# Later lists, the last two chunks sum by sum, and the entrance of Mamba-2 in the kernel of the 304 token columns

## The chip, the cores and the metric

The kernel is one launch on one core of a Trainium2 chip. The metric is device time in microseconds (us), the median of the runs shown. The engines are named as the profile names them: PE (the matrix engine; PEld is its weight load), DVE (vector), ACT (activations and casts), POOL (GpSimd) and SP (which issues DMAs).

## The reference

One inference step of a two-layer trunk: RWKV-7, then PEER, then Mamba-2, then PEER, each added to the residual h. A prompt of 256 tokens with 16 meta tokens ahead and 8 samples of 4 tokens share the weights, so 304 columns go through. All is float32; D is 1024. The parts that the change touches: per token and head, PEER takes 16 of 128 keys in two halves (`P_TOPK`), then 16 of their sums, each one of 16384 experts; in Mamba-2 (`ssd`), `Lmat` is what the kernel calls the score tiles E:

```python
def peer_ffn(xn, w_q, sub_keys, u_tab, v_tab):
    ...
    q = (xt @ w_q).reshape(T, P_HEADS, 2, P_QDIM // 2)
    s = jnp.einsum('thzd,zhkd->thzk', q, sub_keys).astype(F32)
    sv, si = lax.top_k(s, P_TOPK)     
    cand = sv[:, :, 0, :, None] + sv[:, :, 1, None, :]
    ...
    top_s, pos = lax.top_k(cand.reshape(T, P_HEADS, P_TOPK * P_TOPK), P_TOPK)
    eidx = jnp.take_along_axis(cand_idx.reshape(T, P_HEADS, P_TOPK * P_TOPK), pos, axis=-1)
    gate = jax.nn.softmax(top_s, axis=-1).astype(xn.dtype)
    ...
        u = u_tab[i_blk]
        v = v_tab[i_blk]
        act = jax.nn.gelu(jnp.einsum('td,ted->te', x_blk, u), approximate=False)
        return jnp.einsum('te,ted->td', g_blk * act, v)

def ssd(x, dt, A, Bm, Cm, h0, lead_pad, chunk):
    ...
    adt = jnp.moveaxis(dt * A, 2, -1)
    Lmat = jnp.exp(segsum(adt))
    cb = jnp.einsum('bclgn,bcsgn->bcgls', Cm, Bm)
    y_diag = jnp.einsum('bcgls,bcgrls,bcsgrp->bclgrp', cb, Lmat, xdt)
    decay_st = jnp.exp(a_cs[..., -1:] - a_cs)
    ...
```

## The kernel before

**Layout.** The residual is h[128, 8, 304]: 8 blocks of 128 features, 304 token columns. `trunk` runs rwkv, peer of layer 0, mamba and peer of layer 1 one after the other. The two peer phases are recorded in a block that the scheduler orders by a simulated timeline, and Mamba-2's instructions can also be emitted in another order than written; what is passed to `keep_in_program_order` stays in the order of the code with its like.

**Products.** Every float32 product is split in a high part (cast) and a remainder. `load_w` (L293) fetches 128x1024 weights into `wraw` (3 buffers); `split` (L276) has ACT cast them to `whi` (L279), and the remainder `wlo` is taken by POOL (L284) for the first `leng` of 8 blocks and by DVE (L286) for the rest; `whi` and `wlo` have two buffers each. `mm3` (L301) issues 16 products, whi by the high and the low part of x in turn (L305, L306), and then 8 of wlo by the high part (L308), all into one sum. In the rows, `psc` is the sum of a u product, `xh` and `xl` the two parts of x.

**PEER.** All 16384 experts are computed for the 256 prompt tokens, in 128 u products of 256 columns (`s_chunk`, L1075), each with a Gelu on ACT. Beside the first 56 of them (B0) runs the selection `topk` on DVE, one step after each u product and two after every other: token group 0 (samples and meta), then 1 and 2 (128 prompt tokens each). Its rows bear the name G, since its scratch lies in that tensor: MAX8 at L993, the elementwise steps at L1007 to L1009, the sums at L1016 and L1017. The three last steps of a group are held in `late` and issued after the u product that a table names:

```python
        AFTER = ((14, 16, 55), (29, 31, 39), (46, 46, 52))
        for b in range(B0):
            s_chunk(b, G[:, b], leng=LP if b < LB else None, tag="so"[b % 2])
            next(tk, None)
            ...
                    if b == AFTER[ti][i]:
                        late[ti][i]()
```

These are `exps` (ACT, L1019), `gates` (DVE, L1022 to L1024), and for the prompt groups `finish`: three transposes `ptk` on PE (L1029) and a copy to the list `sel` on ACT; for group 0 it is `indices`, which writes the lists out by DMA. All 56 u products take the whole remainder on POOL (LP = 8).

**One-hots.** Then, for four tokens at a time, `onehots` (L1104) makes `oa` (on ACT, POOL or DVE by a pattern of letters) and `ob` (DVE, L1109) from `sel`, three buffers deep, so three groups can be made ahead; PE multiplies them (`pwt`, L1135) into the gates by expert, and DVE and ACT multiply G by these (L1136, L1137). Ten more u products are threaded through.

**v.** 128 chunks follow (L1248). Each has 12 products of 512 columns (L1288) into four sums `acc0` to `acc3`: sum i is token half i // 2 and feature half i % 2. Within a chunk come whi by gh (the high part of G) for the four sums, whi by glo, and wlo by gh; in chunk 127 the twelve are sorted by sum. At the end of layer 0 each sum is copied (ACT for even i, DVE for odd i), transposed on PE (`pot`, L1314) and added to h on DVE; in layer 1 the sums are normed and written out.

**Mamba-2.** `mamba` (L1321) fetches three blocks of the input weights (40, 32, 36). `pre` (L1351) splits two of them ahead with `load_w`, whose remainders go to POOL as a whole (LE = 8). `prenorm` (L333) makes xh and xl from h before the norm's factor is known (xl on DVE, L339), and then calls `rmsnorm` (squares on ACT and DVE, L319; the factor `rr`, L329), in whose middle block 40 is multiplied. `decays` makes from it the running sums of log decays (a chain on DVE), `ec` (L1472), whose product is `pcd`, and the 24 score tiles (L1482 to L1495): `rh` on POOL (L1489), two products `pe` on PE (L1492, and L1493 with the mask `mk`) and Exp on ACT (L1494). The projections and convolutions (`xc`, with Silu on ACT) run between them. `mk` is cast on DVE in two pieces: the identity at L1340 and the two masks at L1418.

Of the kernel before, what the change touches and what calls it, by code (L numbers as in the profile page):

```python
# [23 lines left out]
F32 = mybir.dt.float32  # L24
F32R = mybir.dt.float32r
# [12 lines left out]
KB = 8  # L38
# [28 lines left out]
def chain(*gens):  # L67
    for g in gens:
        yield from g
# [157 lines left out]
class K:  # L227
# [102 lines left out]
        for k in range(KB) if out is not None else ():  # L330
            nc.vector.scalar_tensor_tensor(out[:, k], h[:, k], self.vec(g, k), ri, op0=ALU.mult, op1=ALU.mult)

    def prenorm(self, out, h, g, xh, xl, sq, rr, tag, mid):  # L333

        nc = self.nc
        for k in range(KB):
            x = nc.scalar.activation(xh[:, k], h[:, k], AF.Copy, scale=self.vec(g, k))
            self.tc.keep_in_program_order(x)
            nc.vector.scalar_tensor_tensor(xl[:, k], h[:, k], self.vec(g, k), xh[:, k].bitcast(F32), op0=ALU.mult, op1=ALU.subtract)  # L339
        self.rmsnorm(out, h, g, sq, None, tag, rr, mid)  # L340
        return rr[1]

# [508 lines left out]
    def peer(self, l, ng):  # L851

        nc, tc, a, C, V = self.nc, self.tc, self.a, self.C, self.nc.vector
# [67 lines left out]
        for ti, slot in ((1, B0 + 8), (2, B0 + 16), (0, B0)):  # L921
            c0, c1 = TS[ti]
            n = c1 - c0
# [132 lines left out]
        def gather_u(gs):  # L1056

            for g in gs:


                xr = hs[:, 512 + 1024 * (g % 2):1536 + 1024 * (g % 2)]
                nc.sync.dma_start(xr, xd[16 * g:16 * g + 16, None, :].to_broadcast([16, 8, D]))
                yield
                for m in range(16):
                    rows = gview(slot(), (128, D))
                    nc.gpsimd.indirect_dma_start(out=rows, out_offset=None, in_=a[f"un{l}"],  # L1066
                                                 in_offset=bass.IndirectOffsetOnAxis(ap=gi[:, 0, g, m:m + 1], axis=0))
                    late_u.append((rows, xr, g, m))
                    if len(late_u) > LG:
                        dot(*late_u.pop(0))  # L1070
                    yield
            for x in late_u:
                dot(*x)
# [13 lines left out]

        tk = chain(topk(0), topk(1), topk(2))

        AFTER = ((14, 16, 55), (29, 31, 39), (46, 46, 52))  # L1090
        for b in range(B0):
            s_chunk(b, G[:, b], leng=LP if b < LB else None, tag="so"[b % 2])
            next(tk, None)
# [142 lines left out]
        def slot():  # L1236
# [5 lines left out]
            used[r] = now[1]  # L1242
            return 4 * r

        ggen = chain(gather_u(range(ng)), gather())
        nleft = 128 - B0 - NF
        done = 0
        for b in range(128):  # L1248
# [32 lines left out]

            vhf, vlf = (w.rearrange("p k d -> p (k d)") for w in (vh, vl))
            todo = [(i, g, w) for g, w in ((gh, vhf), (gl, vhf), (gh, vlf)) for i in range(4)]
            if b == 127:
                todo.sort(key=lambda x: x[0])
            for i, g, w in todo:
                t0, d0 = i // 2 * 128, i % 2 * 512
                mm(acc[i], lhsT=g[:, t0:t0 + 128], rhs=w[:, d0:d0 + 512], start=b == 0 and g is gh and w is vhf,  # L1288
# [14 lines left out]
        for i, pt in enumerate(self.gpt):  # L1303
            hk = self.h[:, 4 * i:4 * i + 4, 0:16 * ng].rearrange("p k (g t) -> p k g t", t=16)
            V.tensor_add(hk, hk, pt.rearrange("p k (g t) -> p k g t", t=32)[:, :, 0:ng, 0:16])
        for i in range(4):
            ot = gview(100 + 2 * i, (128, 512))
            if i % 2:
                V.tensor_copy(ot, acc[i])
            else:  # L1310
                nc.scalar.copy(ot, acc[i])
            pt = self.bank([128, 4, 128], "pot", "s")
            for j in range(4):
                mm(pt[:, j], lhsT=ot[:, j * 128:(j + 1) * 128], rhs=C["eye"], is_transpose=True, start=True, stop=True)  # L1314
            t0 = 48 + i // 2 * 128
            hk = self.h[:, i % 2 * 4:i % 2 * 4 + 4, t0:t0 + 128]
            V.tensor_add(hk, hk, pt)
# [3 lines left out]
    def mamba(self):  # L1321
# [15 lines left out]
        tok = pp.tile([128, 3, 128], F32, name="tok")  # L1337
        cdb = pp.tile([128, 10, 32], F32, name="cdb")
        mk = pp.tile([128, 3, 128], BF, name="mk")
        V.tensor_copy(mk[:, 2], C["eye"])  # L1340
        self.psum(i=2, G=2, f=2, t=2)
        ep = st.enter_context(tc.tile_pool(name="ep", bufs=4, reuse_waits="tile"))

# [4 lines left out]
        LE = 8  # L1348
        NU = 4
        done = [0]  # L1350
        pre = {b: self.load_w(a["win"][b], leng=LE, raw=raws[b]) for b in (40, 32)}  # L1351
        xn = ep.tile([128, KB, T], F32, name="xn", tag="E")
        rr = ep.tile([128, 2, T], F32, name="rr", tag="E")

        def proj(blk):

            if done[0] and blk == 40:
                return first.pop()
            w = pre.pop(blk) if blk in pre else self.load_w(a["win"][blk], leng=LE if done[0] < LM else None,
                                                                    raw=raws.get(blk))  # L1360
            c0 = M0 if blk < 16 else 0
            p = self.bank([128, T - c0], "pi", "i" if done[0] % NU < 2 or done[0] >= NU else "f")
            if done[0] == NU:
                with tc.high_priority(offset=200):
                    for k in range(KB):
                        self.split(xh[:, k], xl[:, k], xn[:, k])
            done[0] += 1
            self.mm3(p, w, (xh[:, :, c0:], xl[:, :, c0:]))
            return p

        first = []
        ri = self.prenorm(xn, self.h, "nm1", xh, xl, ep.tile([128, KB, T], F32, name="sq", tag="E"), (rr[:, 0], rr[:, 1]), "t",
                          lambda: first.append(proj(40)))
        gp = st.enter_context(tc.tile_pool(name="mg", bufs=2, reuse_waits="tile"))

        def conv(blk):
# [32 lines left out]
        def decays(dp):  # L1409
# [6 lines left out]
            x = t384("x"); xs = t384("xs")[:, 0:T]  # L1416
            V.tensor_mul(xs, p, ri)
            tc.keep_in_program_order(V.tensor_copy(mk[:, 0:2], nm))  # L1418
            p = xs
            for dst, src in ((x[:, 0:96].rearrange("p (c t) -> p c t", t=32), p[:, None, 16:48].to_broadcast([128, 3, 32])),  # L1420
                             (x[:, 96:128], p[:, 0:32]), (x[:, 128:384], p[:, 48:T])):
# [298 lines left out]
```

## Time and profile before

| | |
|---|---|
| median of 3 runs | 2630.28 us (2629.93 to 2636.83) |
| profiled execution | 2634.19 us, span 2632.3 us |
| granted TensorE clock, mean | 0.974 |
| busy PE | 2477.9 us (94%) |
| busy PEld | 2137.4 us (81%) |
| busy DVE | 1898.8 us (72%) |
| busy ACT | 1253.6 us (48%) |
| busy POOL | 1008.2 us (38%) |
| DMA | 460.34 MB, 175 GB/s over the span |

A share is busy time by the span, an average over stages with different limits. Rows of the trace give the start in us from the span's beginning, the duration, engine, line, operation, output <- inputs (buffer numbers left out), sizes, and how many alike follow each other (x8; the duration is then the sum); in brackets stands how long the engine had waited just before, and for which instruction. Rows of the waits give the total in us, how many and the longest.

### The profile page before, as it was taken

What the parts mean: (1) busy time and instruction counts of PE and PEld (TensorE: products, weight loads), DVE (VectorE), ACT (ScalarE), POOL (GpSimd) and SP (SyncE); (2) the same over time, 40 slices, a digit from 0 to 9 for tenths busy, and PEclk for the clock granted to TensorE, in tenths of its full rate; (3) what the DMA queues carried; (4) which work ended last, traced back from release to release, by engine and by line L of the source; (5) the groups of instructions that cost most, each with busy time, mean ns of one, the idle gap of its engine ahead of it and who ended that gap; (6) DMA issues with size and microseconds to landing.
All of it is one profiled execution on the core that took longest, in us unless ns stands there. A gap on an engine that the chain in (4) does not pass through costs nothing. (4 is left out here: it accounts for less than half of the span.)

```text
span 2632.3 us, 47459 instructions
## 1 busy us (share of the span) xinstructions
PE 2477.9 (94%) x18281; PEld 2137.4 (81%) x18281; DVE 1898.8 (72%) x3724; ACT 1253.6 (48%) x2384; POOL 1008.2 (38%) x863
## 2 busy tenths in 40 slices
PE   7999999996989999999978988999889899999998
PEld 4677768996978888888864886989789788888886
DVE  5355556797695678788784887769949756776777
ACT  3322223453784444444456543335448644444444
POOL 4111110495980233533146555117769401223210
PEclk9999999998999999999989999999989999999999
DMA  3111115453416788888732443555543267787774
GB/s 142 51 45 50 47 55 170 141 183 121 134 40 215 250 312 309 299 306 299 273 110 80 156 164 118 160 177 154 168 122 98 84 213 257 255 285 268 261 265 157
DMA packets 125858, 460.34 MB, mean 175 GB/s; under 512 B 14816, under 2 KB 15744, under 8 KB 122432
## 3 DMA queue, kind: packets, MB, share of 16 engines
q1 hardware_dynamic: 99488, 360.75, 42.1%
q0 software_dynamic: 26144, 96.56, 10.2%
q8 instruction: 144, 2.36, 0.4%
q14 instruction: 82, 0.67, 0.1%
HBM read 440.70 MB, written 16.56 MB: 174 GB/s over the span
## 5 line engine op out<-in xcount | busy, mean ns | idle before, releaser
L279 ACT CAST whi<-wraw 128x1024 fp32r<-128x1024 f32 (+1 forms) x619 | 642.1, 1038 | 870.7 <-PE acc L1288 312.9
L286 DVE TENSOR_TENSOR wlo<-wraw,whi 128x1024 fp32r<-128x1024 f32 (+1 forms) x493 | 593.7, 1204 | 397.2 <-ACT whi L279 339.6
L305 PE MATMUL psc<-xh,whi 128*128 128x256 f32 x2048 | 506.6, 285 | 3.1 <-ACT h L1080 2.6
L306 PE MATMUL psc<-xl,whi 128*128 128x256 f32 x2048 | 504.8, 283 | 0.0
L284 POOL TENSOR_TENSOR wlo<-wraw,whi 128x1024 fp32r<-128x1024 f32 (+1 forms) x150 | 355.1, 2374 | 176.5 <-ACT whi L279 91.0
L305 PEld LDWEIGHTS psc<-xh,whi 128*128 128x128 f32 x2048 | 388.0, 189 | 10.0 <-ACT h L1080 3.1
L306 PEld LDWEIGHTS psc<-xl,whi 128*128 128x128 f32 x2048 | 388.6, 190 | 5.5
L1066 POOL DMA_INDIRECT G<-in_un,gi x80 | 114.5, 1432 | 468.5 <-DVE glo L286 304.6
L1288 PE MATMUL acc<-whi,glo 128*128 128x512 f32 x1024 | 285.1, 399 | 6.7 <-DVE glo L286 6.7
L308 PE MATMUL psc<-xh,wlo 128*128 128x256 f32 x2048 | 290.3, 283 | 0.0
L1288 PE MATMUL acc<-whi,gh 128*128 128x512 f32 x1024 | 283.9, 398 | 1.9 <-ACT gh L279 1.0
L1288 PE MATMUL acc<-wlo,gh 128*128 128x512 f32 x1024 | 281.8, 397 | 0.0
L308 PEld LDWEIGHTS psc<-xh,wlo 128*128 128x128 f32 x2048 | 263.0, 188 | 0.5 <-issue 0.3
L1288 PEld LDWEIGHTS acc<-whi,glo 128*128 128x128 f32 x1024 | 193.8, 190 | 54.8 <-DVE glo L286 7.6
L1288 PEld LDWEIGHTS acc<-wlo,gh 128*128 128x128 f32 x1024 | 192.7, 189 | 47.8 <-DVE wlo L286 1.3
L1163 POOL DMA_INDIRECT G<-in_v,gi x80 | 117.0, 1463 | 298.2 <-DVE G L1158 163.8
L1288 PEld LDWEIGHTS acc<-whi,gh 128*128 128x128 f32 x1024 | 185.0, 189 | 40.3 <-ACT whi L279 1.6
L1135 PE MATMUL pwt<-ob,oa 128*128 128x128 f32 x1024 | 144.8, 282 | 11.6 <-DVE ob L1109 7.8
L1135 PEld LDWEIGHTS pwt<-ob,oa 128*128 128x128 f32 x1024 | 127.8, 191 | 23.2 <-issue 19.3
L305 PE MATMUL pi<-xh,whi 128*128 128x304 f32 (+1 forms) x328 | 102.5, 331 | 11.7 <-ACT xh L279 3.7
L286 DVE TENSOR_TENSOR glo<-G,gh 128x256 fp32r<-128x256 f32 x256 | 106.9, 419 | 2.7 <-ACT gh L279 2.7
L279 ACT CAST gh<-G 128x256 fp32r<-128x256 f32 x256 | 101.8, 399 | 11.7 <-PE acc L1288 11.6
(484 smaller groups left out, 4444.0 us busy)
## 6 DMA issues: line engine op xcount, KB each, us to landing
wraw<-in_u SPq DMA_DIRECT2D x256, 512.0 KB
wraw<-in_v SPq DMA_DIRECT2D x256, 512.0 KB
wraw<-in_win SPq DMA_DIRECT2D x41, 512.0 KB
wraw<-in_wq SPq DMA_DIRECT2D x32, 512.0 KB
wraw<-in_rkv SPq DMA_DIRECT2D x24, 512.0 KB
h<-in_ssm SPq DMA_DIRECT2D x8, 1024.0 KB
out_sssm<-h POOLq DMA_DIRECT2D x8, 1024.0 KB
wraw<-in_wo SPq DMA_DIRECT2D x8, 512.0 KB
```

The costliest lines, as they stand in the source:

```text
L279: self.nc.scalar.copy(hi, x)
L284: self.nc.gpsimd.tensor_sub(lo[:, :n], x[:, :n], hi[:, :n].bitcast(F32))
L286: self.nc.vector.tensor_sub(lo[:, n:], x[:, n:], hi[:, n:].bitcast(F32))
L305: nc.tensor.matmul(ps, lhsT=whi[:, k], rhs=xhi[:, x0 + k], start=start and k == 0, stop=False)
L306: nc.tensor.matmul(ps, lhsT=whi[:, k], rhs=xlo[:, x0 + k], start=False, stop=False)
L308: nc.tensor.matmul(ps, lhsT=wlo[:, k], rhs=xhi[:, x0 + k], start=False, stop=stop and k == kb - 1)
L1066: nc.gpsimd.indirect_dma_start(out=rows, out_offset=None, in_=a[f"un{l}"], in_offset=bass.IndirectOffsetOnAxis(ap=gi[:, 0, g, m:m + 1], ax ...
L1135: mm(pw[:, j], lhsT=oa[:, j], rhs=ob[:, j], start=True, stop=True)
L1163: nc.gpsimd.indirect_dma_start(out=rows, out_offset=None, in_=vrows, in_offset=bass.IndirectOffsetOnAxis(ap=gi[:, 1, g, m:m + 1], axis=0))
L1288: mm(acc[i], lhsT=g[:, t0:t0 + 128], rhs=w[:, d0:d0 + 512], start=b == 0 and g is gh and w is vhf, stop=b == 127 and w is vlf)
```

## The change

Four things are done.

1. **AFTER.** `finish` of group 1 is issued after u product 52 instead of 39; `exps` and `gates` of group 2 after 45 instead of 46; its `finish` after 55 instead of 52. Group 0 and the rest keep their places.
2. **The last two chunks of v.** The products of chunk 126 are held back, and issued with those of 127, sorted by sum. The order of the sums, ORD, is 0, 2, 1, 3 in layer 0 and 0, 1, 2, 3 in layer 1; the copies at the end of layer 0 go by it too, ACT and DVE in turn.
3. **Mamba-2's first two remainders.** `pre` now has only the casts on ACT; the two remainders are taken on DVE by `lows`, which `prenorm` calls behind xl.
4. **mk.** The cast of the identity is written in `decays` behind that of the masks, no longer at the head of `mamba`.

```diff
-    def prenorm(self, out, h, g, xh, xl, sq, rr, tag, mid):
+    def prenorm(self, out, h, g, xh, xl, sq, rr, tag, mid, then=None):
...
             nc.vector.scalar_tensor_tensor(xl[:, k], h[:, k], self.vec(g, k), xh[:, k].bitcast(F32), op0=ALU.mult, op1=ALU.subtract)
+        if then is not None:
+            then()
         self.rmsnorm(out, h, g, sq, None, tag, rr, mid)
...
-        AFTER = ((14, 16, 55), (29, 31, 39), (46, 46, 52))
+        AFTER = ((14, 16, 55), (29, 31, 52), (45, 45, 55))
...
+        ORD = (0, 1, 2, 3) if last else (0, 2, 1, 3)
...
             todo = [(i, g, w) for g, w in ((gh, vhf), (gl, vhf), (gh, vlf)) for i in range(4)]
-            if b == 127:
-                todo.sort(key=lambda x: x[0])
+
+            if b == 126:
+                kept = todo
+                todo = []
+            elif b == 127:
+                todo = sorted(kept + todo, key=lambda x: ORD.index(x[0]))
...
-        for i in range(4):
+        for n, i in enumerate(ORD):
             ot = gview(100 + 2 * i, (128, 512))
-            if i % 2:
+            if n % 2:
                 V.tensor_copy(ot, acc[i])
...
-        V.tensor_copy(mk[:, 2], C["eye"])
...
-        pre = {b: self.load_w(a["win"][b], leng=LE, raw=raws[b]) for b in (40, 32)}
+        pre = {}
+        for b in (40, 32):
+            pre[b] = tuple(self.wp.tile([128, KB, 128], F32R, name=n, tag=n) for n in ("whi", "wlo"))
+            nc.scalar.copy(pre[b][0], raws[b])
+
+        def lows():
+            for b in (40, 32):
+                tc.keep_in_program_order(V.tensor_sub(pre[b][1], raws[b], pre[b][0].bitcast(F32)))
...
-                          lambda: first.append(proj(40)))
+                          lambda: first.append(proj(40)), lows)
...
             tc.keep_in_program_order(V.tensor_copy(mk[:, 0:2], nm))
+            V.tensor_copy(mk[:, 2], C["eye"])
```

What this moves on the engines is shown at three places, each before and then with the change. Lines behind prenorm are a few higher in the changed kernel (L1029 is L1031 there, L1494 is L1509).

The first place is PE in layer 0, at the list of group 1: a u product's last rows, the transposes `ptk` and the beginning of the next u product. G is the tensor whose scratch holds the list, c0 the identity.

```order
L306 MATMUL psc_6883<-xl_4614,whi_6879 128x256
L308 MATMUL psc_6883<-xh_4613,wlo_6880 128x256 x8
L1029 MATMUL ptk_6923<-c0_67,G_4612 128x128 x3
L305 MATMUL psc_6934<-xh_4613,whi_6930 128x256
L306 MATMUL psc_6934<-xl_4614,whi_6930 128x256
```

With the change:

```order
L306 MATMUL psc_7326<-xl_4614,whi_7322 128x256
L308 MATMUL psc_7326<-xh_4613,wlo_7323 128x256 x8
L1031 MATMUL ptk_7352<-c0_67,G_4612 128x128 x3
L305 MATMUL psc_7363<-xh_4613,whi_7359 128x256
L306 MATMUL psc_7363<-xl_4614,whi_7359 128x256
```

`ptk` stands behind product 52 and no longer behind 39, with 13 more u products ahead of it on PE; that of group 2 follows three products further on. On DVE the gates of group 2 stand ahead of the first group of one-hots, where three groups stood ahead of them.

The second place is DVE at the entrance of Mamba-2, up to the normed block `xn`. `sq` are the squares' sums, `rr` the norm's factor.

```order
L1340 CAST mk_14010<-c0_67 128x128
L339 SCALAR_TENSOR_TENSOR xl_14002<-h_64,vecs_69,xh_14001 128x304 x8
L319 TENSOR_TENSOR sq_14029<-sq_14029 128x304 x6
L329 RECIPROCAL rr_14028<-rr_14028 128x304
L331 SCALAR_TENSOR_TENSOR xn_14027<-h_64,vecs_69,rr_14028 128x304 x8
```

With the change:

```order
L1433 CAST mk_14010<-c0_67 128x128
L339 SCALAR_TENSOR_TENSOR xl_14002<-h_64,vecs_69,xh_14001 128x304 x8
L1364 TENSOR_TENSOR wlo_14019<-wraw_13990,whi_14018 128x1024
L1364 TENSOR_TENSOR wlo_14022<-wraw_13992,whi_14021 128x1024
L319 TENSOR_TENSOR sq_14026<-sq_14026 128x304 x6
L329 RECIPROCAL rr_14025<-rr_14025 128x304
L331 SCALAR_TENSOR_TENSOR xn_14024<-h_64,vecs_69,rr_14025 128x304 x8
```

The two remainders stand between xl and the squares; the cast of `mk`, written later in the code, still stands first.

The third place is ACT among the score tiles: `xc` and `zs` belong to the first state group's convolutions and gates, `cdb` and `tok` are the copies of `pcd` and `ptok`, and ACT_TABLE_LOAD is the loading of another table of functions.

```order
L1401 ACTIVATE xc_14489<-ac_14484 128x256
L1494 ACT_TABLE_LOAD
L1494 ACTIVATE E_14513<-pe_14522 128x512
L1475 COPY cdb_14009<-pcd_14178 128x320
L1479 COPY tok_14008<-ptok_14181 128x384
L1494 ACTIVATE E_14513<-pe_14528 128x512
L1647 ACT_TABLE_LOAD
L1647 ACTIVATE zs_14665<-pi_14704 128x288
L1638 COPY xt_14278<-px_14495 128x512
L1638 COPY xt_14278<-px_14501 128x512
L1494 ACT_TABLE_LOAD
L1494 ACTIVATE E_14513<-pe_14534 128x512
```

With the change:

```order
L1509 ACTIVATE E_14513<-pe_14522 128x512
L1509 ACTIVATE E_14513<-pe_14528 128x512
L279 CAST whi_14796<-wraw_14794 128x1024
L279 CAST whi_14869<-wraw_14867 128x1024
L1490 COPY cdb_14009<-pcd_14178 128x320
L1494 COPY tok_14008<-ptok_14181 128x384
L1509 ACTIVATE E_14513<-pe_14534 128x512
L1653 COPY xt_14278<-px_14495 128x512
L1653 COPY xt_14278<-px_14501 128x512
L1509 ACTIVATE E_14513<-pe_14540 128x512
L1653 COPY xt_14278<-px_14507 128x512
L1509 ACTIVATE E_14513<-pe_14546 128x512
```

From the third tile on the tiles and the copies `xt` follow one another with no load of a table between them; `zs` stands behind the tiles. On PE the fourth tile's product stands ahead of `pcd`, and 20 tiles behind it.

## The prediction

> **What bounds the kernel now.** The waits of PE come first, then a table of stretches around the longest of them, then the rows of PE, POOL and DVE inside it. PE is busy for 94% of the span, so time can only come out of the few places where PE stands. The columns of the wait table are: who waits, for what, microseconds in total, times, longest.
>
> ```profile
> PE ptk L1029 <- DVE G L1024: 20.5, 2, 10.2
> PE ptk L1029 <- DVE G L1016: 19.3, 2, 9.8
> PE ptk L1029 <- DVE G L1017: 3.0, 1, 3.0
> PE pe L1492 <- POOL rh L1489: 7.0, 3, 2.8
> PE pi L306 <- DVE xl L339: 3.8, 1, 3.8
> ```
>
> The first three rows are one event in each of the two PEER layers: the transposes of the selected lists (ptk) wait for the selection on DVE. Together 42.8 us. The other two belong to Mamba-2. The table of stretches (PE, weight load, DVE, ACT, POOL busy, then clock, DMA share, GB/s) shows layer 0 around that wait:
>
> ```profile
> 541.00:607.00 66.00, 66.00 (x557) 66.00 (x556) 66.00 (x193) 33.82 (x50) 60.81 (x24) 1.00 0.60 186
> 607.00:629.00 22.00, 1.96 (x11) 1.44 (x10) 21.96 (x43) 1.33 (x3) 2.68 (x2) 0.60 0.18 58
> 700.00:740.00 40.00, 38.57 (x335) 38.24 (x334) 39.64 (x98) 35.99 (x106) 37.30 (x41) 1.00 0.30 95
> ```
>
> Before the wait PE and DVE are both full and POOL nearly so. In the wait DVE works alone: PE, ACT and POOL hold 2 us or less each. In the one-hot stage (700 to 740) everything is full again. PE's rows:
>
> ```profile
> 603.56 1.11 PE L308 MATMUL psc<-xh,wlo 128*128 128x256 f32 x8
> 606.42 1.11 PE L308 MATMUL psc<-xh,wlo 128*128 128x256 f32 x8
> 617.43 0.47 PE L1029 MATMUL ptk<-c,G 128*128 128x128 f32 x1 [9.80 <-DVE G L1016]
> 628.15 0.47 PE L1029 MATMUL ptk<-c,G 128*128 128x128 f32 x1 [10.24 <-DVE G L1024]
> 628.27 0.56 PE L305 MATMUL psc<-xh,whi 128*128 128x256 f32 x1
> 631.83 1.13 PE L308 MATMUL psc<-xh,wlo 128*128 128x256 f32 x8
> ```
>
> One u product takes 2.86 us (603.56 to 606.42), and PE stands from about 607.4 to 628.2. The 16 products behind the wait take 3.56 us (628.27 to 631.83) where 2.86 - 0.95 = 1.91 is usual: the slow clock after the stand costs another 1.65. So a layer loses 20.8 + 1.65 = 22.4 us here.
>
> **The lists moved to later u products.** ptk of the first 128 tokens goes from behind product 39 to behind product 52, that of the others from 52 to 55. 13 products are 13 x 2.86 = 37 us, so PE would come to it at 607.4 + 37 = 644.5. Is DVE ready by then? In the wait it ran without POOL, and unwaited PE calls POOL's remainder (wlo) in every product. What that does to DVE, from the POOL row and the rows of DVE on both sides:
>
> ```profile
> 607.78 2.35 POOL L284 TENSOR_TENSOR wlo<-wraw,whi 128x1024 fp32r<-128x1024 f32 x1 [0.45 <-ACT whi L279]
> ```
>
> ```profile
> 585.97 3.43 DVE L1007 TENSOR_TENSOR G<-G 128x1920 bf16<-128x1920 bf16 x1
> 594.02 2.48 DVE L978 CAST G<-G 128x256 bf16<-128x256 uint32 x1
> 600.38 2.05 DVE L987 TENSOR_TENSOR G<-G 128x120 bf16<-128x120 bf16 x1
> 603.80 1.05 DVE L1008 TENSOR_TENSOR G<-G 128x128 f32<-128x128 f32 x1
> 604.77 0.28 DVE L1017 TENSOR_TENSOR G<-G 128x128 f32<-128x128 f32 x1
> 606.41 1.07 DVE L1009 SCALAR_TENSOR_TENSOR G<-G 128x128 f32<-128x128 f32 x1
> 607.41 0.98 DVE L993 MAX8 G<-G 128x8 f32<-128x50 f32 x8
> 620.49 1.22 DVE L1007 TENSOR_TENSOR G<-G 128x1920 bf16<-128x1920 bf16 x1
> 624.68 0.28 DVE L1008 TENSOR_TENSOR G<-G 128x128 f32<-128x128 f32 x1
> 629.26 2.29 DVE L1016 TENSOR_REDUCE G<-G 128x128 f32<-128x2048 bf16 x1
> 631.46 0.76 DVE L1109 TENSOR_TENSOR ob<-cp,sel 128x512 f32<-128x512 f32 x1
> 636.23 2.43 DVE L1120 TENSOR_SCALAR oa<-cp,sel 128x128 f32<-128x128 f32 x1
> 676.04 1.35 DVE L1109 TENSOR_TENSOR ob<-cp,sel 128x256 f32<-128x256 f32 x1 [0.27 <-PE pwt L1135]
> ```
>
> L1007 takes 3.43 us beside POOL and 1.22 without it, L1008 1.05 and 0.28: an elementwise operation of DVE waits for the end of a running POOL operation. With 0.28 as the bare time of a small one, the first six rows wait 2.2, 2.2, 1.8, 0.8, 0 and 0.8: 1.3 on average. From 607.41 to the end of the row at 629.26 are 24.1 us, the gates of the last list add 0.6, and 13 more elementwise operations now lie beside POOL. Bounds: no wait gives 607.4 + 24.7 = 632, a whole POOL operation each (2.35) gives 663. I take 1.3, which is what the nearest rows show: 16.9 us, so DVE is through at 649.
>
> The Trainium skill, page "SBUF — State Buffer", section "Who interferes with whom", has a rule that speaks against this change: VectorE and GpSimd share one pair of ports, and whichever of a two-input VectorE operation and a GpSimd operation starts second is blocked for the whole of the other. The L1007 pair agrees with it. Taken strictly, each of the 13 could pay up to a full POOL operation, the upper bound and the second rival below.
>
> Next is late what stood ready before: three groups of one-hots (631.46 to 638.66, 7.2 us) were made while PE still ran u products. Now they start at 649, with the last full remainder of POOL (2.35) between, and end at 658.6. Before, DVE began the fourth group at 676.04. So layer 0 gains 676.0 - 658.6 = 17.4 of the 22.4 that PE loses; PE would come to the one-hots at about 652 and wait a few us. DVE, POOL and ACT are full in that stage (row 700 to 740), so a later start of DVE isn't made up, and this is also why the gain isn't 22.4. In layer 1 DVE is 3.0 us further behind (the L1017 row): 14.4. **Sum 31.8**; bounds 4.6 (a full POOL operation each: 13 x 1.05 = 13.7 less per layer, below zero only with the fourth rival) and 47.8 (22.4 + 25.4).
>
> **Mamba-2.** Two remainders go from POOL to DVE behind xl; by the orders shown above, the cast of mk, although written later, still stands first on DVE.
>
> ```profile
> 1331.13 4.67 POOL L284 TENSOR_TENSOR wlo<-wraw,whi 128x1024 fp32r<-128x1024 f32 x2
> ```
>
> ```profile
> 1331.56 2.01 DVE L1340 CAST mk<-c 128x128 bf16<-128x128 f32 x1
> 1333.49 5.75 DVE L339 SCALAR_TENSOR_TENSOR xl<-h,vecs,xh 128x304 fp32r<-128x304 f32 x8
> 1398.78 0.21 DVE L1472 TENSOR_TENSOR ec<-ch,cm 32x64 f32<-32x64 f32 x1
> ```
>
> With POOL silent the cast needs about 0.28 (1.7 less) and xl loses up to one POOL wait (0 to 2.3); the two remainders add 2 x 1.2 (1204 ns, the L286 group of the page) ahead of the squares. Net gain 1 (-0.7 to 1.6); PE's wait of 3.8 for xl shrinks with it. The larger effect is in the order: the 24 score tiles E run nearly in one piece, without the table loads between.
>
> ```profile
> 1432.62 1.02 PE L1492 MATMUL pe<-rh,L 128*128 128x512 f32 x2
> 1434.92 1.03 PE L1492 MATMUL pe<-rh,L 128*128 128x512 f32 x2
> 1438.00 1.23 PE L308 MATMUL pi<-xh,wlo 128*128 128x288 f32 x8
> ```
>
> ```profile
> L1489 POOL TENSOR_TENSOR rh<-R,cm 128x512 f32<-128x512 f32 x24 | 28.5, 1198 | 11.1 <-PE pe L1492 8.9 <-DVE R L1452 2.1
> L1494 ACT ACT_TABLE_LOAD x4 | 5.1, 1283 | 0.1
> ```
>
> In a run a tile costs 1.15 us (two in 2.30). From ec to the last remainder are 1438.0 - 1399.0 = 39 us now. After it 20 tiles are left behind ec: 23 us, and four products of POOL between at 1.2: 4.8. That is 11 less; the transposes and copies for the first state group then stand behind the tiles (about 2 to 3). I take 8, bounds 0 (the chain to ec comes later by as much) and 11. **Mamba-2 together 9**, bounds -1 to 13.
>
> **End of v.** The sums finish in the order 0, 2, 1, 3 in layer 0, but by the order of instructions still within the last four products, since these wait for wlo. One gap is there to win:
>
> ```profile
> 1329.68 1.21 PE L1314 MATMUL pot<-c,G 128*128 128x128 f32 x8 [0.48 <-ACT whi L279]
> ```
>
> I cost it at nothing, bounds 0.5 either way. In layer 1 only the first eight of product 126 change places: nothing.
>
> **Sum.** 31.8 + 9 + 0 = 41 us. The profiled execution took 2634.2 (span 2632.3): 2593. The median of the runs shown is 3.9 lower, 2630.3, so I forecast **2589 us**.
>
> **The rivals.**
> - *DVE keeps up* (13%): the waits behind POOL cost nothing, as in the L1017 row; PE finds lists and one-hots ready. 47.8 + 9 = 57: 2573. Against it: five of the six rows beside POOL waited.
> - *A full POOL operation each* (15%): 4.6 + 9 = 14: 2617. For it: L1007, L978 and L987 waited nearly a whole one; against it the three others.
> - *Mamba-2 gives nothing* (12%): the chain on DVE up to ec is no shorter, and what is moved behind the tiles comes back as waits in the first state group. 32: 2598.
> - *Slower* (5%): the entry of the one-hot stage, on DVE. If the waits of 2.35 go on through its first operations too, about five more than the rows at 631 to 638 had, DVE gets to the fourth group at 658.6 + 13.7 + 11.8 = 684, 8 later than before, in layer 1 11: 19 - 9 = 10 slower, 2640. It decides from a mean wait of 2.3 us over these 18 operations.
> - *The gain isn't one* (5%): the stage behind is full on four engines and its end is set elsewhere, so PE only waits later; Mamba-2 alone: 2621. For the end of v and mk this is already so by the order.
>
> **How the numbers follow.** The forecast has 50%. About 0.3% (8 us) is what a measurement of this kernel can tell from no change. Faster by more: forecast, the first three rivals and a part of the last, 91%; slower by more 4%; within it 5%. From 2572 to 2617 the forecast and the first three rivals are in, 90% by these chances, of which I trust 80, the unknown being the mean wait.
>
> **What would show it.** Right: no PE wait for ptk above 5 us in either layer; the DVE rows of the selection beside running POOL rows, ended near 649; DVE's fourth group near 659 and PE waits for ob or oa of a few us at the start; 20 score tiles at 1.15 us. Wrong: ptk still waiting by tens of us (the order isn't what runs), POOL's remainders late for PE in the u products, or the one-hot stage longer by as much as the u products became shorter.

## The result, and the profile after

| | median (runs) | against before |
|---|---|---|
| before, beside the first runs | 2631.5 us (2629.9 to 2636.8, 4) | |
| changed kernel, first runs | 2590.1 us (2586.6 to 2593.7, 4) | 0.9839, 95% interval 0.9817 to 0.9861 |
| changed kernel again, with more runs | 2588.0 us (2587.0 to 2591.8, 5) | 0.9823, 95% interval 0.9809 to 0.9836 |

The change makes the kernel faster by 41.5 us in the first set and by 47.7 in the second (before had 2635.6 there). The forecast was 2589 us, 41 below before, within 2572 to 2617.

First the waits of PE in the changed kernel (who waits, for what, microseconds in total, times, longest):

```profile
PE pi L308 <- DVE wlo L286: 8.7, 3, 3.0
PE pwt L1137 <- DVE ob L1111: 8.0, 32, 1.3
PE psn L321 <- DVE sq L319: 7.3, 2, 7.1
PE ptk L1031 <- DVE G L1026: 6.2, 2, 4.9
PE pwt L1137 <- DVE ob L1120: 3.0, 1, 3.0
PE pe L1507 <- POOL rh L1504: 3.0, 2, 2.3
```

Of 42.8 us at the transposes `ptk`, 6.2 are left in two waits, one of 4.9 in layer 1 and the other of 1.3 in layer 0. In Mamba-2 the wait for xl at the entrance (3.8) is gone and that for `rh` is 3.0 where it was 7.0; against that, PE now waits 8.7 us for remainders by DVE (L286) where it was 4.3. The stretches of layer 0 (columns as before the change):

```profile
603.00:640.00 37.00, 36.22 (x300) 35.59 (x300) 36.97 (x41) 19.18 (x28) 34.99 (x13) 1.00 0.57 175
640.00:652.00 12.00, 10.16 (x84) 9.72 (x83) 11.90 (x8) 8.14 (x20) 11.61 (x8) 1.00 0.44 129
```

While DVE ends the selection, PE now has u products (36.22 of 37), and POOL their remainders (34.99), where PE and POOL stood before. PE's and DVE's rows there:

```profile
481.40 0.36 PE L305 MATMUL psc<-xh,whi 128*128 128x256 f32 x1
643.52 0.33 PE L1031 MATMUL ptk<-c,G 128*128 128x128 f32 x1 [1.30 <-DVE G L1026]
654.50 1.80 PE L1137 MATMUL pwt<-ob,oa 128*128 128x128 f32 x7 [3.05 <-DVE ob L1120]
764.03 0.83 PE L1137 MATMUL pwt<-ob,oa 128*128 128x128 f32 x6
```

```profile
616.18 2.27 DVE L1018 TENSOR_REDUCE G<-G 128x128 f32<-128x2048 bf16 x1
631.97 2.29 DVE L1019 TENSOR_TENSOR G<-G 128x128 f32<-128x128 f32 x1
634.18 2.48 DVE L1011 SCALAR_TENSOR_TENSOR G<-G 128x128 f32<-128x128 f32 x1
641.02 2.45 DVE L1026 TENSOR_TENSOR G<-G 128x128 f32<-128x128 f32 x1
643.39 3.42 DVE L1017 TENSOR_TENSOR G<-G 128x2048 bf16<-128x2048 bf16 x1
649.59 2.37 DVE L1026 TENSOR_TENSOR G<-G 128x128 f32<-128x128 f32 x1
651.88 0.68 DVE L1111 TENSOR_TENSOR ob<-cp,sel 128x512 f32<-128x512 f32 x1
```

Steps that took 0.28 or 0.29 us in the stand of PE (L1017, L1009 and L1024 before, now L1019, L1011 and L1026) take 2.3 to 2.5 with POOL at work beside them. DVE comes to the one-hots at 651.88, and PE waits 3.05 us for `ob` at its first product of one-hots. From the first u product (481.40) to the end of the last product of one-hots (764.86) are 283.5 us.

The same stretch can be measured in each profiled execution, and so can others: end of the last `pot` to the first u product of layer 1 (Mamba-2 with the queries of layer 1), first to last product of v, and the time up to the first u product, which the change doesn't touch. All in us:

| execution | to first u | layer 0: u to one-hots | v 0 | Mamba-2 and queries | layer 1: u to one-hots | v 1 |
|---|---|---|---|---|---|---|
| before | 485.6 | 298.2 | 543.1 | 442.1 | 301.1 | 546.2 |
| changed | 481.4 | 283.5 | 544.3 | 434.7 | 284.1 | 546.8 |
| changed, again | 483.4 | 283.4 | 541.5 | 433.5 | 281.2 | 546.4 |
| lists alone | 479.6 | 282.9 | 544.4 | 446.7 | 281.4 | 546.5 |
| Mamba-2 alone | 481.7 | 298.2 | 546.6 | 430.6 | 301.5 | 545.1 |
| v alone | 481.9 | 298.5 | 544.9 | 445.8 | 301.4 | 546.9 |
| no remainders 40 to 55 | 481.9 | 271.5 | 545.1 | 427.6 | 271.4 | 547.5 |
| list at 46 | 480.3 | 290.3 | 544.2 | 429.0 | 293.5 | 545.5 |
| halves | 482.8 | 284.9 | 544.3 | 433.9 | 284.2 | 545.8 |
| halves, lists sooner | 482.1 | 283.3 | 542.0 | 433.9 | 282.9 | 544.8 |
| halves from product 38 | 481.7 | 282.9 | 544.1 | 435.1 | 282.5 | 545.5 |
| remainders on POOL in Mamba-2 | 483.7 | 283.8 | 543.7 | 443.5 | 280.0 | 546.8 |
| 58 u products ahead | 480.4 | 284.8 | 536.6 | 428.1 | 289.7 | 541.0 |
| 60 u products ahead | 480.6 | 289.1 | 536.2 | 432.3 | 291.7 | 537.3 |

Columns that a kernel doesn't change scatter: the start by 6 us, v 0 by 5, the Mamba-2 column by 5 to 8. The two PEER columns hardly scatter where the kernel is that of before (298.2 to 298.5, 301.1 to 301.5). A part of the scatter goes with the granted clock, which the profile gives for each stretch: up to the first u product it was 0.99 in before's execution (485.6 us) and 1.00 in that with the lists alone (479.6); over the Mamba-2 column it was 0.92 in the two longest executions (446.7 and 445.8) and 0.95 in those of 429.0 and 428.1.

### The profile page after: what moved, and what is told of

Its sections match the earlier page's. It is cut to its first block, busy times and chain, and to the rows that moved or that the text cites. A ratio compares the mean times of both kernels' runs of the same rounds, so it can differ in the third digit from the quotient of the medians.

```text
span 2590.7 us, 47466 instructions
## 1 busy us (share of the span) xinstructions
PE 2472.6 (95%) x18281; PEld 2130.9 (82%) x18281; DVE 1923.0 (74%) x3726; ACT 1245.9 (48%) x2378; POOL 1027.4 (40%) x861
## 3 DMA queue, kind: packets, MB, share of 16 engines
q1 hardware_dynamic: 99488, 360.75, 42.8%
q8 instruction: 144, 2.36, 0.4%
## 5 line engine op out<-in xcount | busy, mean ns | idle before, releaser
L286 DVE TENSOR_TENSOR wlo<-wraw,whi 128x1024 fp32r<-128x1024 f32 (+1 forms) x493 | 590.3, 1198 | 371.8 <-ACT whi L279 317.2
L284 POOL TENSOR_TENSOR wlo<-wraw,whi 128x1024 fp32r<-128x1024 f32 (+1 forms) x148 | 364.4, 2473 | 154.6 <-ACT whi L279 96.7
L1295 PEld LDWEIGHTS acc<-whi,glo 128*128 128x128 f32 x1024 | 193.4, 189 | 54.6 <-DVE glo L286 7.6
L286 DVE TENSOR_TENSOR glo<-G,gh 128x256 fp32r<-128x256 f32 x256 | 107.0, 419 | 2.7 <-ACT gh L279 2.7
```

What stands on the lines that cost most here:

```text
L284: self.nc.gpsimd.tensor_sub(lo[:, :n], x[:, :n], hi[:, :n].bitcast(F32))
L286: self.nc.vector.tensor_sub(lo[:, n:], x[:, n:], hi[:, n:].bitcast(F32))
```

## The experiments

**The parts alone.** The new AFTER table in the kernel before:

```diff
-        AFTER = ((14, 16, 55), (29, 31, 39), (46, 46, 52))
+        AFTER = ((14, 16, 55), (29, 31, 52), (45, 45, 55))
```

> The kernel before with the new AFTER table alone. Theory (the lists are the bulk): of the 41 us between the two medians this part gives 32, so about 2600 us (ratio 0.988); the profiles of before and after put 14.8 and 17.1 on the two stretches from the first u product to the end of the one-hots. Rival 1 (PE only waits later): 2625 or more. Rival 2 (the whole gain is here and Mamba-2 gives nothing): 2590.

Measured: 2598.3 us beside 2633.2, ratio 0.9861 (0.9843 to 0.9879), so 34.8 us. The two stretches give 15.4 and 19.7, together 35.1: the whole gain is there.

Then the entrance of Mamba-2 alone (`prenorm` with `then`, `lows`, and the cast of `mk` in `decays`, as in the change):

> The kernel before with the entrance of Mamba-2 alone (two remainders on DVE behind xl, the cast of mk written later). Theory: 7 us less, by the stretch from the end of layer 0 to the end of Mamba-2 in the two profiles: about 2624. Rival (nothing): 2631. Within it: the squares' product psn comes 2 to 3 us earlier, the rest appears between ec and the first state group.

Measured: 2621.2 us, ratio 0.9952 (0.9935 to 0.9969), so 11.9 us and more than the 7 that one pair of profiles gave. The pair was misleading, as the column of Mamba-2 shows: its four executions with the remainders on POOL take 442.1 to 446.7, the ten with the new entrance 427.6 to 435.1, and the pair was the shortest of the one kind and nearly the longest of the other. The clock alone doesn't make the difference: at the same 0.93 it takes 442.1 and 443.5 with the remainders on POOL and 430.6 and 433.9 with the new entrance.

Then the last two chunks of v alone:

> The kernel before with the last two chunks of v sum by sum alone. Forecast: nothing, 2631, bounds 0.5 either way. The profiles put the stretch of v 1.2 us (layer 0) and 0.6 us (layer 1) longer after the change; rival: these belong to this part, then 2633. Further question: before's profile takes 4.2 us longer than after's up to the first u product, where the change touches nothing; if this profile differs there as well, it is scatter between executions, not the change.

Measured: 2632.5 us, ratio 1.0001 (0.9988 to 1.0014): nothing, as forecast; and its start took 481.9, so the 485.6 of before's profiled execution is that execution's own, with its lower clock.

The changed kernel was then run once more:

> The changed kernel once more beside the same runs of before. The lists alone gave 34.8 us by the medians and Mamba-2 alone 11.9; if the parts add up, this one lies 44 to 47 us under before (ratio 0.982 to 0.983); if the parts take something from each other, about 41 (0.9844), as in its first runs. Up to the first u product its profile should take 481 to 482 us, like the others' after before's 485.6.

Measured: 2588.0 beside 2635.6, ratio 0.9823 (0.9809 to 0.9836): 47.7 us, where the parts sum to 34.8 + 11.9 = 46.7. The parts add up. Its profile took 483.4 to the first u product, outside the 481 to 482 that was expected there.

**What the waits behind POOL cost.** In the changed kernel, u products 40 to 55 get no remainder (POOL has nothing to do there, and whi is multiplied again in its place, so that part of the product is left out):

```diff
+            if 40 <= b < B0:
+                hi = self.wp.tile([128, 8, 128], F32R, name="whi", tag="whi")
+                nc.scalar.copy(hi, self.fetch(a[f"u{l}"][b]))
+                w = hi, hi
```

> The changed kernel, in which u products 40 to 55 of both layers have no remainder: POOL is silent there, and whi is multiplied a second time in place of wlo (that part of the product is left out). Theory (DVE's elementwise steps wait for POOL's running remainder): the rows L1017, L1019, L1011, L1026 of the selection, which take 3.42, 2.29, 2.48 and 2.45 us beside POOL after the change, fall to 1.22, 0.28, 0.29 and 0.29; the gates of the last list end about 24 us sooner, no wait for ptk is left, and the time falls by 3 to 8 us per layer at most, as PE had waited only 6.2 there: 2575 to 2585. Rival (those rows are long by themselves beside a busy PE and the DMA): the durations stay, and so does the time, 2590.

Measured: 2566.7 us, ratio 0.9745 (0.9731 to 0.9758), 21 below the changed kernel and more than expected. DVE's rows of this kernel at the same place:

```profile
609.00 2.27 DVE L1018 TENSOR_REDUCE G<-G 128x128 f32<-128x2048 bf16 x1
618.96 0.28 DVE L1019 TENSOR_TENSOR G<-G 128x128 f32<-128x128 f32 x1
619.16 0.28 DVE L1011 SCALAR_TENSOR_TENSOR G<-G 128x128 f32<-128x128 f32 x1
621.69 0.28 DVE L1026 TENSOR_TENSOR G<-G 128x128 f32<-128x128 f32 x1
621.90 1.21 DVE L1017 TENSOR_TENSOR G<-G 128x2048 bf16<-128x2048 bf16 x1
625.89 0.29 DVE L1026 TENSOR_TENSOR G<-G 128x128 f32<-128x128 f32 x1
643.14 0.69 DVE L1116 TENSOR_TENSOR ob<-cp,sel 128x512 f32<-128x512 f32 x1 [16.96 <-ACT sel L1034]
```

Every long row of the changed kernel is back at its bare length, beside the same u products on PE: it is POOL that they wait for. The gates end at 626.2 (625.89 + 0.29) where they ended at 652.0 (649.59 + 2.37). A TENSOR_REDUCE takes 2.27 in both. What the run doesn't separate: without POOL's remainders, both lists' products and more of POOL's own work come ahead of the one-hot stage too, so the 12 us per layer (283.5 to 271.5) are the price of those remainders as a whole, not of DVE's waits alone. By the trace 5.8 of them lie ahead of DVE's fourth group of one-hots, which begins 170.0 us behind the first u product instead of 175.8, and 6.2 behind it.

**The place of the wait.** The list of group 1 asked for behind product 46:

```diff
-        AFTER = ((14, 16, 55), (29, 31, 52), (45, 45, 55))
+        AFTER = ((14, 16, 55), (29, 31, 46), (45, 45, 55))
```

> The changed kernel with the list of group 1 asked for behind u product 46 instead of 52. Theory: PE comes to it 17 us sooner (6 products), waits until DVE has it, and in that time POOL is silent, so DVE runs on at its bare durations; PE stands 7 to 9 us longer per layer (1.65 of it the slow clock) and DVE then waits for PE, as before the change: 12 to 18 us more than the changed kernel, about 2604. Rival (the place of the wait doesn't matter, since DVE sets the end of the stage and gains while PE stands): within 4 us of it, 2590.

Measured: 2603.3 us, ratio 0.9883 (0.9868 to 0.9898), 15.3 above the changed kernel of the same runs. PE's and DVE's rows of this kernel:

```profile
632.36 0.47 PE L1031 MATMUL ptk<-c,G 128*128 128x128 f32 x1 [9.19 <-DVE G L1026]
```

```profile
629.30 0.28 DVE L1019 TENSOR_TENSOR G<-G 128x128 f32<-128x128 f32 x1
636.22 0.30 DVE L1026 TENSOR_TENSOR G<-G 128x128 f32<-128x128 f32 x1
659.84 0.69 DVE L286 TENSOR_TENSOR wlo<-wraw,whi 128x512 fp32r<-128x512 f32 x1 [16.31 <-PE psc L308]
```

While PE stands (9.19), DVE runs at 0.28 again and has the lists done at 636.5, 156.2 us behind the first u product where the changed kernel needs 170.6; then it stands 16.31 itself. What DVE gains in the stand of PE is of no use afterwards. The stretches are 6.8 and 9.4 to 12.3 longer. The theory holds, the rival falls. (This varies the place of group 1's list alone; no run moves that of group 2 by itself.)

**Smaller instructions on POOL.** The remainders of the first 56 u products in two instructions of four blocks:

```diff
+                for i in range(0, 8, 4):
+                    nc.gpsimd.tensor_sub(w[1][:, i:i + 4], raw[:, i:i + 4], w[0][:, i:i + 4].bitcast(F32))
```

> The changed kernel, in which POOL takes the remainder of the first 56 u products in two instructions of four blocks each instead of one of eight; nothing is left out. Theory (a DVE step waits for the end of POOL's running instruction): a wait is at most half as long, the rows L1019, L1011, L1026 and L1017 of the selection's end fall by about half (2.45 to 1.2 and less, 3.42 to about 2.3), the gates of the last list end 8 to 12 us sooner and the time falls by 5 to 10 us per layer: 2570 to 2580. Rival (POOL's next instruction is let in ahead of DVE, or POOL slows down and PE waits for remainders): the same time or longer.

Measured: 2593.7 us, ratio 0.9837 (0.9824 to 0.9851), by the medians 5.8 above the changed kernel; the intervals overlap, so that it is slower isn't settled, but the 5 to 10 us per layer of the theory aren't there. Rows of DVE, and a row of PE's waits, of this kernel:

```profile
614.85 1.18 DVE L1019 TENSOR_TENSOR G<-G 128x128 f32<-128x128 f32 x1
615.95 1.38 DVE L1011 SCALAR_TENSOR_TENSOR G<-G 128x128 f32<-128x128 f32 x1
620.55 1.35 DVE L1026 TENSOR_TENSOR G<-G 128x128 f32<-128x128 f32 x1
621.83 2.32 DVE L1017 TENSOR_TENSOR G<-G 128x2048 bf16<-128x2048 bf16 x1
```

```profile
PE psc L308 <- POOL wlo L1084: 8.1, 13, 1.3
```

The mechanism is as the theory has it: the rows are about half as long (2.29 to 1.18, 2.45 to 1.35). The price isn't. DVE is let in twice as often, and POOL pays for it; the groups of POOL's remainders from 603 to 634 us, of the changed kernel and then of this one (count, busy us and mean ns of one):

```profile
L284 POOL TENSOR_TENSOR wlo<-wraw,whi 128x1024 fp32r<-128x1024 f32 x11 | 32.4, 2982 | 1.2 <-ACT whi L279 1.2
```

```profile
L1084 POOL TENSOR_TENSOR wlo<-wraw,whi 128x512 fp32r<-128x512 f32 x19 | 30.7, 1652 | 1.5 <-ACT whi L1082 1.5
```

A product's remainder takes 2 x 1.65 = 3.3 us instead of 2.98, PE uses one up in 2.86, and waits 8.1 us where the changed kernel waited 1.5.

Two more runs tried to use the freed time of DVE. Halves throughout, with the lists at ((14, 16, 55), (29, 31, 49), (42, 42, 53)):

> The kernel with the remainders in halves and the lists asked for sooner, to use the DVE time that the halves free: group 1's list behind u product 49, group 2's Exp and gates behind 42 and its list behind 53. In the run with halves DVE had both lists' steps done about 16 us ahead of their places and then stood, and PE waited 8.1 us for late halves of remainders. Theory: the halves' cost stays (8 us) and the earlier lists give back at most what PE still waited at the lists and the first one-hots (6.2 and 3.0) and what DVE stood: between 2578 and 2588. Rival (the end of the one-hot stage is set by DVE's and POOL's work in it alone, so that lists ready sooner give nothing): 2594, as the halves gave.

Measured: 2589.2 us, ratio 0.9831 (0.9816 to 0.9846), just above the theory's range. And halves from product 38 on, with ((14, 16, 55), (29, 31, 50), (43, 43, 55)):

> As the run before, but with halves only from u product 38 on, where the long elementwise steps of DVE stand; group 1's list behind 50, group 2's Exp and gates behind 43, its list behind 55. Theory: PE's waits for remainders fall to about half of 8.1 us and most of DVE's 16 us stay: 2575 to 2585, below the changed kernel's 2588. Rival: 2588 or more, since what DVE gains is not on the path.

Measured: 2587.1 us, ratio 0.9821 (0.9804 to 0.9838), again above the theory's range and as good as at its rival's 2588. Both are level with the changed kernel. Their lists are ready about 10 us sooner (DVE's first one-hot 158 and 160 us behind the first u product, against 170.5), and the stretches are 283.3 and 282.9 in layer 0: nothing of it arrives at the end of the one-hots. The traces show why: PE is no sooner there. It waits 9.0 and 6.7 us (both layers together) for the halves and comes to its first product of one-hots 171.5 and 172.8 us behind the first u product, 173.1 in the changed kernel; DVE's fourth group, which needs the buffer of a group that PE has multiplied, begins at 172.6 and 174.8, against 175.8.

**Mamba-2's remainders back on POOL**, at the place where the change puts them:

```diff
-                tc.keep_in_program_order(V.tensor_sub(pre[b][1], raws[b], pre[b][0].bitcast(F32)))
+                tc.keep_in_program_order(P.tensor_sub(pre[b][1], raws[b], pre[b][0].bitcast(F32)))
```

> The changed kernel with Mamba-2's first two remainders back on POOL, at the place in the code where the change puts them. The order of the score tiles is then that of before, with table loads between. Theory (taking them off POOL does it: mk and xl no longer wait, and the tiles come in one piece): Mamba-2 falls back to its length before, 390 to 396 us from the end of layer 0 to the norm of layer 1's PEER against 377 to 383, so about 12 us more than the changed kernel. Rival (their place behind xl does it): no more than 3 us.

Measured: 2598.6 us, ratio 0.9858 (0.9842 to 0.9873), 10.7 above the changed kernel: the gain of Mamba-2 is gone, and the lists' is left (0.9861 in the run with the lists alone). DVE's rows at the entrance, in the changed kernel and then in this one:

```profile
1313.81 0.22 DVE L1433 CAST mk<-c 128x128 bf16<-128x128 f32 x1
1313.94 3.65 DVE L339 SCALAR_TENSOR_TENSOR xl<-h,vecs,xh 128x304 fp32r<-128x304 f32 x8
1317.51 2.36 DVE L1364 TENSOR_TENSOR wlo<-wraw,whi 128x1024 fp32r<-128x1024 f32 x2
1319.79 2.40 DVE L319 TENSOR_TENSOR sq<-sq 128x304 f32<-128x304 f32 x6
```

```profile
1315.87 1.98 DVE L1433 CAST mk<-c 128x128 bf16<-128x128 f32 x1
1317.77 5.76 DVE L339 SCALAR_TENSOR_TENSOR xl<-h,vecs,xh 128x304 fp32r<-128x304 f32 x8
1323.45 5.32 DVE L319 TENSOR_TENSOR sq<-sq 128x304 f32<-128x304 f32 x6
```

The cast of `mk` stands at the same place in both: its move does nothing, POOL's silence shortens it from 1.98 to 0.22. The other half of the gain is the order of the score tiles, which the scheduler makes and which goes back with the remainders; the two can't be told apart by this run.

**More u products ahead of the one-hots.** B0 = 58 with the lists behind 54 and 57:

> The changed kernel with 58 instead of 56 u products ahead of the one-hots and the lists two products later (54 and 57). Theory (PE's remaining waits at the lists and the first one-hots, about 6 us in layer 0, are filled with products that would else run in the stage of v): 2580 to 2584. Rival (DVE falls behind by the two further remainders of POOL, 2 x 1.3 to 2.4, and the one-hots end as much later): 2588 to 2592.

Measured: 2579.1 us (2577.2 to 2587.8), ratio 0.9800 (0.9780 to 0.9819). Of PE's waits at `ptk` one of 1.4 is left, in layer 1. By the medians it is 8.8 below the changed kernel, but the intervals overlap, and the table gives less: v is shorter by 5 to 8 and by 5 to 6 (two products fewer in it), the u stretch of layer 0 1.3 longer, that of layer 1 5.6 to 8.4 longer. Between nothing and 6 us are left, and the rest lies in the Mamba-2 column, which this edit doesn't touch. And B0 = 60 with the lists behind 54 and 57:

> As the run with 58 u products ahead of the one-hots, but with 60; the lists stay behind products 54 and 57. With 58 no wait for a list was left on PE. Theory (only PE's waits were filled, and they are used up): two more products ahead only move work to where PE is full as well: 2577 to 2582, the same as with 58. Rival (DVE ready with lists and one-hots still waits for PE in the one-hot stage, or the stage gets shorter with fewer products in the last part): 2573 or less; rival on the other side (POOL's two further remainders hold up DVE): 2584 or more.

Measured: 2582.6 us, ratio 0.9803 (0.9777 to 0.9829), no better than 58. Both medians lie below that of the changed kernel; that either is faster than it isn't settled.

## Why the prediction was right, step by step

The place and the mechanism were right. That the time came out within about 1 us of the forecast both times is in part luck. The first runs gained 41.5 where 41 were forecast, but the second set gained 47.7 and the parts 46.7; in that set the time still fits, since before took 2635.6 there and not the 2630.3, from three runs, that the forecast started from. Within the lists' term the errors of the two layers cancelled in part.

**The bound and the place.** Right: PE's stand at `ptk` was the loss, and the gain lies where it was said to: of 46.7 us by the parts, 34.8 in the two PEER stretches (forecast 31.8), 11.9 in Mamba-2 (9), nothing in v (0).

**The waits behind POOL.** The mechanism and the count were right, the size wasn't. Between MAX8 and the last gate, 13 rows of DVE are longer in the changed kernel than in the run without remainders, by 25.5 us in all (0.28 to 2.29, 1.21 to 3.42 and so on): 1.96 each, where 1.3 was taken from six rows ahead of the stand, and 2.35 was the upper bound. So DVE's first one-hot comes 170.5 us behind the first u product; the forecast of 649 in before's trace was 163.4 behind it. The 7.1 between them are nearly 13 x 0.66 = 8.6, less 1.7 that the sum had twice: POOL isn't busy for "2 us or less" in the stand but for 2.68, with the remainder at 607.78, and the 24.1 us from 607.41 already hold the wait of L1011 for it (3.96 at 608.31, 2.29 at 625.60). The six rows were drawn mostly from a time when DVE's searches (MAX8 and the like, whose times don't change) lay between the elementwise steps; at the end of the selection these steps follow each other, and POOL is busy for 34.99 of 37 us. Before's trace held such a case too: from 585.97 on L1007, L1036, L1037 and L978 follow each other and take 3.43, 2.42, 2.43 and 2.48, and two of these four aren't among the six. That the density makes the difference is argued from these rows, no run varies it alone. By the rule of the Trainium skill ("SBUF — State Buffer", section "Who interferes with whom") this is an exclusive lock that whoever starts first holds for its whole instruction; 1.96 of 2.35 lies nearer to that than to my mean. The same section says that a tensor_reduce never takes part on trn2 and that a cast can, and the runs agree: L1018 takes 2.27 with and without POOL, the cast of `mk` 1.98 and 0.22.

**From the lists to the one-hots.** The forecast let DVE begin the fourth group of one-hots 17.4 us sooner, and took this for the gain of layer 0. The group began 14.7 sooner, counted from the first u product (657.20 - 481.40 = 175.8, before 676.04 - 485.57 = 190.5), and the layer gained 14.8. Its row, and before's two rows of DVE ahead of its own fourth group:

```profile
657.20 0.41 DVE L1111 TENSOR_TENSOR ob<-cp,sel 128x256 f32<-128x256 f32 x1
```

```profile
655.39 0.29 DVE L1022 TENSOR_REDUCE G<-G 128x8 f32<-128x128 f32 x1 [16.74 <-ACT G L1019]
675.08 0.69 DVE L286 TENSOR_TENSOR wlo<-wraw,whi 128x512 fp32r<-128x512 f32 x1 [17.57 <-PE psc L308]
```

Before the change DVE stood for 16.74 and 17.57 us there; with the change its selection, longer by the waits, takes up that time. From the fourth group to the end of the one-hots are 107.8 us before the change and 107.7 after it (in layer 1 107.8 and 107.3): the mark was well chosen, and that the stage behind it makes nothing up was right. The 17.4 was too much by 2.8, from two errors ahead of the mark. DVE reached the first group 7.1 later than forecast; it then made three groups in 5.3 us (651.88 to 657.20) where 9.6 were forecast. The forecast took over two long rows of before (2.45 and 2.43) and put a remainder of 2.35 on top; in the changed kernel POOL issues DMAs from 651.74 to 655.03, and the longest rows of DVE there are 1.29, and 1.54 for two.

**Layer 1.** The step that failed: "In layer 1 DVE is 3.0 us further behind (the L1017 row): 14.4". The gain there is 17.1 in the first profile and 19.7 to 21.1 in the three others with the same lists. The sum took DVE's lag off the gain but left the mark of before where layer 0 has it. In layer 1 before's fourth group stands 2.9 later as well (193.4 us behind the first u product, 190.5 in layer 0), so a lag that stays would have left 17.4. And it doesn't stay. In the changed kernel DVE comes to L1019 6.0 us later behind the first u product than in layer 0, yet to the one-hots at 170.1, against 170.5. The rows of layer 1 show where the lag goes:

```profile
1904.37 0.28 DVE L1019 TENSOR_TENSOR G<-G 128x128 f32<-128x128 f32 x1
1913.72 1.21 DVE L1017 TENSOR_TENSOR G<-G 128x2048 bf16<-128x2048 bf16 x1
1917.72 0.29 DVE L1026 TENSOR_TENSOR G<-G 128x128 f32<-128x128 f32 x1
```

In layer 0 the same steps took 2.29, 3.42 and 2.37, together 6.3 us more. Here no operation of POOL was under way when they began: POOL stands from 1904.10 to 1904.38, from 1913.65 to 1914.81 and from 1917.57 to 1918.81. In the three other executions three or four rows at this place are at their bare length in the same way. The forecast had no such term, and that the lag goes is luck of where the rows fall: with 58 products ahead the lag stays (first one-hot at 170.2 and 176.3), and the gain of layer 1 is 11.5.

**Mamba-2.** Forecast 9, measured 11.9, by these parts (means over the four executions with the remainders on POOL and five with the new entrance, from the changed kernel twice, Mamba-2 alone, list at 46 and halves):

| stretch | forecast | measured |
|---|---|---|
| end of layer 0 to the norm's product psn | 1 sooner | 14.1 to 10.1: 4.1 sooner |
| psn to ec | 0 | 54.8 to 57.0: 2.2 later |
| ec to the last score tile | 8 sooner | 37.8 to 31.0: 6.8 sooner |
| from there to the next norm | 0 | 286.4 to 283.2: 3.2 sooner |

The chain on DVE up to ec gives back half of what the entrance wins; the cause was not tried. In the profiles PE waits 3.05 and 2.65 us for remainders by DVE there, where before it waited 0.38 and 0.98, and the granted clock of this stretch was 0.81 where it was 0.87. At the entrance, xl was expected to lose "up to one POOL wait (0 to 2.3)", and 1 was taken for the net; it lost 2.1 (5.76 to 3.65), the squares 0.8 against the kernel before (3.17 to 2.40), and the cast its 1.8. That is 4.7, of which the two remainders (2.36) take half back; the rest of the 4.1 may come from the granted clock, 0.75 over this stretch in before's profile and 1.00 in that of the changed kernel. The tiles went nearly as worked out: in a run they came every 1.15 us (14 tiles from 1395.83 to 1410.75), but the first of them still waited for POOL. Their group on POOL, in the changed kernel:

```profile
L1504 POOL TENSOR_TENSOR rh<-R,cm 128x512 f32<-128x512 f32 x24 | 25.1, 1049 | 11.8 <-PE pe L1507 10.8 <-DVE R L1467 0.7
```

The mean of `rh` is 1049 ns where it was 1198, and ACT has 2378 instructions where it had 2384: six table loads fewer, all in Mamba-2.

**The rivals.** "A full POOL operation each" was the nearest to what DVE does, with a time 28 us too long: of the wait that it adds a part is made up in the three groups ahead of the mark, and layer 1 skipped some of its waits (its bound of 4.6 is 4.4 by its own terms, 31.8 less twice 13.7). "DVE keeps up" falls by the same rows. "Mamba-2 gives nothing" falls by the run of it alone, "the gain isn't one" by that of the lists alone. For "slower" the waits would have had to go on through the first one-hots; their rows took 0.33 to 1.54 us.

## What to carry to other kernels

A wait of the bounding engine is worth removing by moving the asker behind other work, but the engine that is waited for may have been fast only because the others stood: take its durations from the time in which all of them work, and from the same kind of instruction in the same density. When a gain is read from one mark before and after the change, a lag counts on both sides or on neither. And one pair of profiles gives a term of 10 us only with its scatter: the same stretch in three or four executions of kernels that leave it alone, with its granted clock, shows how much of the difference is the change.

## What the runs showed of the hardware

DVE and POOL pay both ways: a remainder of eight blocks takes POOL 2.35 to 2.40 us where DVE stands or runs only searches, and 2.98 on average beside the end of DVE's selection, and the 13 elementwise steps of DVE there take 1.96 more each on average. Halving POOL's instruction about halved DVE's rows (2.29 to 1.18) and cost POOL a tenth more per product (2.98 to 3.30), enough for PE to wait. Searches and reductions on DVE (MAX8, FIND_INDEX8, TENSOR_REDUCE) took the same time with POOL busy and silent.
